# A seventh weight buffer, and one shift column moved behind the shift of tile 12, in a convolution block on one core

## The chip, the cores and the metric

The kernel runs on one core of one Trainium2 chip. The metric is the device time of one execution in microseconds; the time before is the median of three runs. The profile is one more execution, with its own time.

## The reference, cut to what matters

One decoder layer (depth 1, sequence 256, model width 2048) whose mixer is a causal convolution of width 31, with modulation by a conditioning vector `c`:

```python
cond = silu(c)
sh1, sc1, g1, sh2, sc2, g2 = split(cond @ mod_w + mod_b, 6)
h = rms_norm(x, norm1_g) * (1 + sc1) + sh1
a, gt = split(h @ w_in + b_in, 2)                    # "in":  2048 -> 4096
u = depthwise_conv31(a * sigmoid(gt), dw_w) + dw_b
u = silu(layer_norm(u, ln_g, ln_b))
y = u @ w_out + b_out                                # "out": 2048 -> 2048
x = x + (1 + g1) * y
h = rms_norm(x, norm2_g) * (1 + sc2) + sh2
x = x + (1 + g2) * (square(relu(h @ mlp_w1)) @ mlp_w2)   # "up", "down"
```

All is float32. The kernel multiplies matrices in three passes of a rounded high part and a low part (`hi`, `lo`).

## The kernel before, in words

**Tiles and jobs.** Channels lie on the 128 partitions, 16 tiles of 128 channels, and the 256 tokens lie along the free axis. The matrix work is a list `jobs`: 16 input jobs `("in", i)`, each of which gives one tile `u[i]` (an `a` half and a gate half), 8 output jobs, and the MLP in four quarters of 8 `up` and 8 `down` jobs. In the profile input jobs 8 to 15 end at about 279 us and output job 0 starts at about 304 us. The first eight input jobs run in the opening stage beside the modulation columns.

**Weights.** Every 1 MB weight block is loaded into one of `RAW` buffers named `raw` (128x2048, f32). ACT rounds it to `hi` (L206), and DVE or POOL subtracts to get `lo` (L209). The splits of the input jobs and of the early output block `("out", 1, 0)` go to POOL, those of most others to DVE.

**Modulation.** One `mod_w` block serves either as a row load, `raw<-mod_r`, which PE multiplies by the conditioning vector in 8 matmuls (L310), or as a column load, `raw<-mod_c`, which DVE multiplies and sums in one pass over 2048 elements (`mod_col`, L390), or in two halves (L386) once the output stage has begun. `cols_in` are the first `COLS_IN` columns of the second shift; `late` is the list of the other late rows and columns, dealt to jobs by `LATE_IN` and `LATE_OUT` in `after[job]`.

**Order of loads.** SP issues all loads in one hand-written list `order` (`todo`, `top_up`): for each job the weights of the next job and then what `after` holds for it; at input job 15 it also holds `parts_early` behind that job's successor. `room` bounds how far the list runs ahead of the program, and a load waits in SP's queue until its `raw` buffer is free.

**The convolution.** Eight of the sixteen tiles (`PE_TILES`) are convolved on PE as small diagonal matmuls (`pe_conv`, L735) from a rearranged copy `wide` (`copy_wide`, L710 on DVE and L712 on ACT, nine and seven copies for tiles 14 and 15); the others are taps on DVE (L627), joined by `join` (L630). A common shift is taken out of the convolved tiles before their squares are summed (`add_shift`, L674).

**The end of the input stage (job 15).** The program writes, in this order: the two columns of `cols_in`, held behind the last `join`; the matmuls of job 15; the gate of tile 15 (sigmoid on ACT at L750, product on DVE at L752); its nine and seven copies; the shift of tile 12 (`cvs[3][:, 0:1]`); conv 14 and its statistics (L680); two modulation rows; conv 15; the rest of the statistics; the other seven rows; and then the LayerNorm. For each of eight pairs of tiles the LayerNorm subtracts the mean on POOL (L897), scales on DVE (L898), does the silu on ACT (L902) and splits the result into `hl` (L217 on ACT, and L219 and L220 on DVE). Output job 0 takes these pairs in order as they come. `state["e_end"]` is the DVE instruction behind which columns and DVE's splits of the output weights are put.

Of the kernel before, what the change touches and what calls it, by code (L numbers as in the profile page):

```python
# [11 lines left out]
ALU = mybir.AluOpType  # L12
# [5 lines left out]
KT = D // P  # L18
# [19 lines left out]
ROWS = [nb for g in GROUPS for nb in g]  # L38
COLS = [w * KT + k for k in range(KT) for w in (SC1, SH1)]
COLS += [w * KT + k for w in (SH2, G2) for k in range(KT)]  # L40
RAW = 6
FIRST = 4
PE_TILES = (0, 1, 2, 9, 10, 12, 14, 15)
CONV_AT = {9: (0,), 10: (1,), 11: (2,), 12: (9,), 13: (10,), 14: (12,), 15: (14,)}
ADVANCE = {7: 24, 8: 34, 9: 34, 10: 34, 11: 34, 12: 32, 13: 37, 14: 99}
SHIFT = 2
COPY_AT = {8: 0, 9: 1, 10: 2, 11: 9, 12: 10, 13: 12}
PADDING = 784
UNSHIFTED = 7
LATE_IN = [0] * 8 + [4, 4, 4, 4, 4, 3, 0, 9]  # L50
AHEAD = 2
LATE_OUT = [1, 1, 2, 2, 3, 3, 1, 1]
COLS_IN = 2
URGENT = 400
HELD = 8
EARLY_U = 5
# [10 lines left out]
def conv_block(ctx: ExitStack, tc: tile.TileContext, x, vec, dwq, c_row, mod_r, mod_c, w_first, w_in, w_out, w1, w2, out):  # L67
    nc = tc.nc
# [41 lines left out]
    for i in range(2):  # L110
        p = ps.tile([P, 2, 2 * T], F32, name="mm", bufs=2)
        for n in range(2):
            at = 8 * i + 4 * n
# [4 lines left out]
    state = {"used": 0}  # L118
# [20 lines left out]
    waiting = {"raw": 0, "first": 0, "vec": 0, "x": 0}  # L139
    room = {"raw": RAW + 1, "first": FIRST + 1, "vec": 1, "x": 0}  # L140
    todo = []
# [21 lines left out]
    def home(key):  # L163
        return key[0] if key[0] in ("first", "x", "vec") else "raw"

    def top_up():
        while todo and waiting[home(todo[0])] < room[home(todo[0])]:
            key = todo.pop(0)
            tag = home(key)
            waiting[tag] += 1  # L170
            if tag == "raw":
                raw[key] = wts.tile([P, KT, P], F32, name="raw", bufs=RAW)
            elif tag == "first":
                raw[key] = start_pool.tile([P, 2 * HELD, P], F32, name="first", bufs=FIRST)
            elif tag == "x":
                raw[key] = x_pool.tile([P, KT, T], F32, name="x1")
            else:
                raw[key] = v[:, soon:]
                with tc.issue_after(state["load"].ins):
                    state["load"] = nc.sync.dma_start(dwq_sb, dwq)  # L180
            with tc.issue_after(state["load"].ins) if "load" in state else ExitStack():
                if key in SPLIT_LOADS:
                    first_half = nc.sync.dma_start(raw[key][:, 0:HALF], source(key)[:, 0:HALF])
                    with tc.issue_after(first_half.ins):
                        state["load"] = nc.sync.dma_start(raw[key][:, HALF:], source(key)[:, HALF:])
                else:
                    state["load"] = nc.sync.dma_start(raw[key], source(key))

    def take(key):
        assert order[state["used"]] == key, (order[state["used"]], key)  # L190
        state["used"] += 1
        waiting[home(key)] -= 1
        top_up()
        return raw.pop(key)
# [181 lines left out]
        if which in amps:  # L376
            in_order(lambda: nc.vector.tensor_tensor(amps[which][:, k : k + 1], accs[0], col("n1g", k), op=ALU.mult))

    def mod_col(at):
        w = take(("col", at)).rearrange("p k n -> p (k n)")  # L380
        which, k = divmod(at, KT)
        acc = modc[:, at : at + 1]
        if which == SH2 and "cond" in state:
            n = HALF * P
            for half, total in zip(state["cond"], (acc, rest2[:, k : k + 1])):
                nc.vector.scalar_tensor_tensor(w[:, 0:n], w[:, 0:n], 1.0, half, op0=ALU.mult, op1=ALU.mult, accum_out=total)  # L386
                w = w[:, n:]
            return
        with tc.issue_after(state["e_end"]) if "e_end" in state else ExitStack():
            nc.vector.scalar_tensor_tensor(w, w, 1.0, cb, op0=ALU.mult, op1=ALU.mult, accum_out=acc)  # L390
        if which in amps:
            return nc.vector.scalar_tensor_tensor(
                amps[which][:, k : k + 1], acc, col("modb", at), col("n1g", k), op0=ALU.add, op1=ALU.mult
            )
        elif which != SH2:
            return mod_bias(at, 1, acc)

    def mods(keys):
        for key in keys:
            if key[0] == "mod":  # L400
                mod_chunk(*key[1:])
            else:
                mod_col(key[1])
# [60 lines left out]

    late = [("mod", nb, kg) for nb in ROWS for kg in range(4)] + [("col", SH2 * KT + k) for k in range(COLS_IN, KT)]
    cols_in = [("col", SH2 * KT + k) for k in range(COLS_IN)]
    last = [("col", G2 * KT + k) for k in range(KT)]
# [7 lines left out]
    quota = {("in", i): n for i, n in enumerate(LATE_IN)}  # L475
    quota.update({("out", i): LATE_OUT[i] for i in range(HALF)})
    after = {}
    for job in jobs:
        n = quota.get(job, 0)
        after[job], late = late[:n], late[n:]  # L480
        if job == ("in", KT - 1):
            after[job] = cols_in + after[job]
        if job[:2] in LATE_GATE:
            n = LATE_GATE[job[:2]][job[2]]
            after[job], last = last[:n], last[n:]
# [38 lines left out]
    p = ps.tile([P, 512], F32, name="small", bufs=1)  # L524
    for k2 in range(HALF):
        s = two()
# [8 lines left out]
    with urgent():  # L535
        part = two()[:, 0, :]
        nc.scalar.activation(part, p[:, 0:T], AF.Copy)
        p = ps.tile([P, 512], F32, name="row", bufs=1)
# [8 lines left out]
    for _ in range(2):  # L547
        p = ps.tile([P, 2, 2 * T], F32, name="mm", bufs=2)
# [31 lines left out]
    for k in range(KT):  # L580
# [4 lines left out]
        if c == 0:  # L585
            n = two()
# [18 lines left out]
    cvs = [cvp.tile([P, 4, T], F32, name=f"cv{i}") for i in range(4)]  # L605
# [21 lines left out]
            nc.vector.scalar_tensor_tensor(out, s, w, acc, op0=ALU.mult, op1=ALU.add)  # L627

    def join(out, acc, s):
        state["joined"] = nc.vector.tensor_tensor(out, acc, s, op=ALU.add).ins  # L630

    def conv_steps(ct):
        acc = ps.tile([P, 2, T], F32, name="acc", bufs=2)
# [37 lines left out]

    def add_shift(tiles, n):
        by = state["small"][:, None, T : 2 * T].to_broadcast([P, n, T])
        nc.vector.tensor_tensor(tiles, tiles, by, op=ALU.add)  # L674

    def sum_round(pairs, first=False, last=()):
        for n, tiles in enumerate(zip(*pairs)):
# [38 lines left out]
    def make_diag(ct):  # L716
        diags[ct] = cp.tile([P, 32, 32], F32, name="diag", bufs=2)
        at = PE_TILES.index(ct)
        with tc.issue_after(state["pool"]):
            nc.gpsimd.tensor_tensor(  # L720
                diags[ct],
                col("same", 0, 32)[:, None, :].to_broadcast([P, 32, 32]),
                dwq_sb[:, 32 * at : 32 * at + 32][:, :, None].to_broadcast([P, 32, 32]),
                op=ALU.mult,
            )
# [50 lines left out]
    for n, job in enumerate(jobs):  # L776
        if n < HELD:
            continue
        for ct in CONV_AT.get(n, ()) + ((15,) if n == KT - 1 else ()):
            make_diag(ct)  # L780
        if n < len(jobs) - 1:
            splits(jobs[n + 1])
        if n in COPY_AT:
# [5 lines left out]
        kind, i = job[0], job[-1]  # L789
        if kind == "out" and i > 0:  # L790
            p = ps_two()
        elif not by_tokens(job):
            p = ps.tile([P, 2, 2 * T], F32, name="mm", bufs=2)
# [3 lines left out]
        if job == ("up", 0, 0):  # L797
            mm(p, 0, job + (0,), xa, range(SIDE))
            for at in range(2 * UNSCALED):
                shift_row(at, shown.pop(("up", 0, at // 2, at % 2)))  # L800
            fold_shift()
            mm(p, 0, job + (0,), xa, range(SIDE, KT))
            mm(p, 1, job + (1,), xa)
        elif job in K_OUTER:
            for k2 in range(HALF):
                for c in range(2):
                    mm(p, c, job + (c,), xa if plain else hl, range(2 * k2, 2 * k2 + 2), kind == "out")
        elif kind == "in":
            rows = list(after[job]) if i < KT - 1 else []
            if i == KT - 1:  # L810
                state["e_end"] = state["joined"]
                mods(cols_in)
            for c in range(2) if i < KT - 1 else (1, 0):
                for ks in (range(HALF), range(HALF, KT)):
                    mm(p, c, job + (c,), hl, ks, i == KT - 1)
                    with tc.issue_after(state["mm_end"].ins):
                        mods(rows[:1])
                    del rows[:1]
        elif by_tokens(job):
            mm_tokens(sums[kind, i // 2], job, u2 if kind == "down" else hl, n == len(jobs) - 1)  # L820
        else:
            for c in range(2):
                mm(p, c, job + (c,), hl, merged=kind == "out")
        mod_finish()
        if kind == "in":
# [7 lines left out]
            if n == KT - 2:  # L833
                add_shift(cvs[2][:, 1:3, :], 2)
            if n == KT - 1:
                add_shift(cvs[3][:, 0:1, :], 1)
            for ct in CONV_AT.get(n, ()):
                with tc.issue_after(state["mm_end"].ins):
                    mix(ct)
# [7 lines left out]
            sq15 = two()  # L847
            with tc.issue_after(state["conv_end"].ins):
                stats(2)
            rows = after[job][COLS_IN:]  # L850
            with tc.issue_after(state["stats_end"].ins):
                mods(rows[:AHEAD])
            del rows[:AHEAD]
# [39 lines left out]
            for k2 in range(HALF):  # L893
                e = two()
                f = ps_two()
                with urgent():
                    nc.gpsimd.tensor_tensor(e, pair_of(cvs, k2), spread(mu), op=ALU.subtract)  # L897
                    state["e_end"] = nc.vector.tensor_tensor(e, e, spread(r), op=ALU.mult).ins  # L898
                    for c in range(2):
                        k = 2 * k2 + c  # L900
# [10 lines left out]
            pad = ctx.enter_context(tc.tile_pool(name="pad", bufs=1, side="right"))  # L911
            pad.tile([P, PADDING], F32, name="pad")
            mp = ctx.enter_context(tc.tile_pool(name="mlp", bufs=1, side="right"))
# [5 lines left out]
        if kind == "out":  # L919
# [4 lines left out]
            with urgent():  # L924
                for c in range(2):
                    k = 2 * i + c
# [10 lines left out]
            for c in range(2):  # L937
                k = 2 * i + c
# [27 lines left out]
        elif kind == "up":  # L966
# [3 lines left out]
            if plain:  # L970
                with urgent():
# [3 lines left out]
                    for c in range(2):  # L975
                        at = 2 * i + c
# [13 lines left out]
        else:  # L990
# [13 lines left out]
            for t, cs, p in sums.pop((kind, i // 2)):  # L1004
                at = slice(512 * (i // 2) + cs.start, 512 * (i // 2) + cs.stop)
                s = y[:, t, at]
# [71 lines left out]
```

## Time and profile before

| | us |
|---|---|
| three runs | 1107.52, 1106.05, 1105.78 |
| median | 1106.05 |
| the profiled execution | 1107.45 |
| its span | 1105.7 |
| PE busy | 1086.5 (98%) |
| DVE busy | 746.9 (68%) |
| ACT busy | 509.3 (46%) |
| POOL busy | 194.4 (18%) |
| mean DMA rate | 284 GB/s |

The span is what the profiler recorded between the first and the last instruction; 1.75 us of the profiled execution's time lie outside it. All times in the profile count from the start of the span. PE's work is pipelined, so its busy share says that it nearly always has something to do. The number in brackets at the end of a timeline row is the idle time of the engine ahead of that row, and the instruction that ended it. Engines are PE (matmuls), DVE (vector), ACT (activations), POOL (GpSimd) and SP, which issues the loads.

### The profile page before, as it was taken

What the parts mean: (1) busy time and instruction counts of PE and PEld (TensorE: products, weight loads), DVE (VectorE), ACT (ScalarE), POOL (GpSimd) and SP (SyncE); (2) the same over time, 40 slices, a digit from 0 to 9 for tenths busy, and PEclk for the clock granted to TensorE, in tenths of its full rate; (3) what the DMA queues carried; (4) which work ended last, traced back from release to release, by engine and by line L of the source; (5) the groups of instructions that cost most, each with busy time, mean ns of one, the idle gap of its engine ahead of it and who ended that gap; (6) DMA issues with size and microseconds to landing.
All of it is one profiled execution on the core that took longest, in us unless ns stands there. A gap on an engine that the chain in (4) does not pass through costs nothing.

```text
span 1105.7 us, 15404 instructions
## 1 busy us (share of the span) xinstructions
PE 1086.5 (98%) x6018; PEld 892.9 (81%) x6018; DVE 746.9 (68%) x1023; ACT 509.3 (46%) x679; POOL 194.4 (18%) x119
## 2 busy tenths in 40 slices
PE   7999999999899999999999999999999999999998
PEld 4888876668499998888888888888888888888887
DVE  5777789989666966667875666645656665565653
ACT  4111296664576587444444444433444433444431
POOL 0000176468669343000000000000000000000000
PEclk9999999999999999999999999999999999999999
DMA  9999999976899967889996888857898967788631
GB/s 384 420 421 421 416 375 353 353 287 248 329 362 382 396 242 231 254 270 301 357 412 214 227 255 264 305 153 271 252 237 238 251 204 216 227 240 247 208 105 39
DMA packets 142315, 314.23 MB, mean 284 GB/s; under 512 B 87585, under 2 KB 105505, under 8 KB 107297
## 3 DMA queue, kind: packets, MB, share of 16 engines
q1 hardware_dynamic: 142096, 313.11, 81.0%
q8 instruction: 47, 0.77, 0.3%
q14 instruction: 26, 0.21, 0.1%
q10 hardware_dynamic: 146, 0.13, 0.0%
HBM read 301.15 MB, written 12.07 MB: 283 GB/s over the span
## 4 chain that ended last, share of the span: by engine, by line
PE 85%; DMA 10%; DVE 3%; issue 1%; ACT 0%; SPq 0%; DVEq 0%; ACTq 0%
PE mm L258 20%; PE mm L257 20%; PE mm L259 20%; DMA raw<-mod_c 9%; PE mm L234 6%; PE mm L235 3%; PE acc L231 2%; PE acc L230 2%; PE acc L232 2%; PE row L310 2%; DVE raw L390 2%; PE mm L735 2%; DMA raw<-mod_r 1%; DVE wide L710 1%; DMA x<-x 1%; PE mm L562 1%
## 5 line engine op out<-in xcount | busy, mean ns | idle before, releaser
L206 ACT ACTIVATE hi<-raw 128x1024 fp32r<-128x1024 f32 x320 | 334.9, 1057 | 360.8 <-PE mm L259 324.1
L209 DVE TENSOR_TENSOR lo<-raw,hi 128x1024 fp32r<-128x1024 f32 x257 | 312.0, 1223 | 176.9 <-ACT hi L206 176.3
L258 PE MATMUL mm<-lo,u 128*128 128x512 f32 x496 | 193.0, 389 | 0.0
L257 PE MATMUL mm<-hi,u 128*128 128x512 f32 x496 | 193.0, 389 | 0.0
L259 PE MATMUL mm<-hi,u 128*128 128x512 f32 x496 | 192.9, 389 | 0.0
L209 POOL TENSOR_TENSOR lo<-raw,hi 128x1024 fp32r<-128x1024 f32 x63 | 155.2, 2489 | 199.8 <-ACT hi L206 196.2
L259 PE MATMUL mm<-hi,hl 128*128 128x512 f32 x480 | 186.7, 389 | 0.0
L258 PE MATMUL mm<-lo,hl 128*128 128x512 f32 x480 | 186.7, 389 | 0.0
L257 PE MATMUL mm<-hi,hl 128*128 128x512 f32 x480 | 186.7, 389 | 0.0
L390 DVE SCALAR_TENSOR_TENSOR raw<-raw,cond 128x2048 f32<-128x2048 f32 x51 | 122.6, 2407 | 63.2 <-DMA raw<-mod_c 63.2
L259 PEld LDWEIGHTS mm<-hi,u 128*128 128x128 f32 x496 | 93.1, 188 | 19.3
L258 PEld LDWEIGHTS mm<-lo,u 128*128 128x128 f32 x496 | 93.1, 188 | 19.0
L257 PEld LDWEIGHTS mm<-hi,u 128*128 128x128 f32 x496 | 93.1, 188 | 19.1
L259 PEld LDWEIGHTS mm<-hi,hl 128*128 128x128 f32 x480 | 90.1, 188 | 18.7
L257 PEld LDWEIGHTS mm<-hi,hl 128*128 128x128 f32 x480 | 90.1, 188 | 18.7
L258 PEld LDWEIGHTS mm<-lo,hl 128*128 128x128 f32 x480 | 90.1, 188 | 18.7
L627 DVE SCALAR_TENSOR_TENSOR acc<-u,v,acc 128x256 f32<-128x256 f32 x224 | 94.4, 485 | 1.8
L234 PE MATMUL mm<-hl,hi 128*128 128x512 f32 x224 | 81.5, 405 | 0.0
L562 PE MATMUL mm<-two,first 128*128 128x256 f32 x256 | 60.1, 389 | 8.4 <-ACT two L593 8.3
L562 PEld LDWEIGHTS mm<-two,first 128*128 128x128 f32 x256 | 49.1, 194 | 18.2 <-ACT two L593 11.5
L230 PE MATMUL acc<-hl,hi 128*128 128x256 f32 x224 | 63.4, 283 | 0.0
L231 PE MATMUL acc<-hl,hi 128*128 128x256 f32 x224 | 63.4, 283 | 0.0
(183 smaller groups left out, 1281.1 us busy)
## 6 DMA issues: line engine op xcount, KB each, us to landing
raw<-w SPq DMA_DIRECT2D x128, 1024.0 KB, 5.4
raw<-mod_c SPq DMA_DIRECT2D x62, 1024.0 KB, 9.4
raw<-mod_r SPq DMA_DIRECT2D x32, 1024.0 KB, 7.7
raw<-w_in SPq DMA_DIRECT2D x16, 1024.0 KB, 7.1
raw<-w_out SPq DMA_DIRECT2D x16, 1024.0 KB, 7.9
first<-w_first SPq DMA_DIRECT2D x15, 1024.0 KB, 19.8
flat<-two SPq DMA_DIRECT2D x30, 256.0 KB, 2.8
two<-flat SPq DMA_DIRECT2D x120, 64.0 KB, 4.2
```

Of the source, the lines that this page charges most:

```text
L206: state["w_hi"] = nc.scalar.activation(hi, w[:, ks, :], AF.Copy).ins
L209: end = by.tensor_tensor(lo, w[:, ks, :], hi.bitcast(F32), op=ALU.subtract)
L230: nc.tensor.matmul(out_p, w, m[:, 0:T], start=begin, stop=False)
L231: nc.tensor.matmul(out_p, w, m[:, T : 2 * T], start=False, stop=False)
L234: nc.tensor.matmul(p[:, c, :], hi[:, k % HALF, :], m, start=(k == 0), stop=(k == KT - 1))
L235: state["mm_end"] = nc.tensor.matmul(p[:, c, T : 2 * T], lo[:, k % HALF, :], m[:, 0:T], start=False, stop=(k == KT - 1), skip_group_check= ...
L257: nc.tensor.matmul(p, p_hi, hi, start=begin, stop=False)
L258: nc.tensor.matmul(p, p_hi, lo, start=False, stop=False)
L259: nc.tensor.matmul(p, p_lo, hi, start=False, stop=end)
L390: nc.vector.scalar_tensor_tensor(w, w, 1.0, cb, op0=ALU.mult, op1=ALU.mult, accum_out=acc)
L562: step = nc.tensor.matmul(held[n][:, c, :], w[:, 2 * n + c, :], h, start=k == 0 and c == 0, stop=k == KT - 1, skip_group_check=True)
L627: nc.vector.scalar_tensor_tensor(out, s, w, acc, op0=ALU.mult, op1=ALU.add)
```

## The change

The dynamic scratch of the program is cut from 4096 to 256 bytes and `PADDING` from 784 to 720, and `RAW` goes from 6 to 7. `COLS_IN` goes from 2 to 1, so that the second of the two columns goes to the list `late`; `LATE_OUT` takes it up at output job 3. The remaining column's load moves from the list of input job 15 to the end of that of input job 14, which puts it ahead of the loads of the output weights. Job 15 claims the loaded block early (`taken`), and its product is written behind the shift of tile 12, after which `e_end` also stands.

```diff
-RAW = 6
+RAW = 7
-PADDING = 784
+PADDING = 720
-LATE_OUT = [1, 1, 2, 2, 3, 3, 1, 1]
-COLS_IN = 2
+LATE_OUT = [1, 1, 2, 3, 3, 3, 1, 1]
+COLS_IN = 1
...
-    def mod_col(at):
-        w = take(("col", at)).rearrange("p k n -> p (k n)")
+    def mod_col(at, w=None):
+        w = (take(("col", at)) if w is None else w).rearrange("p k n -> p (k n)")
...
-        if job == ("in", KT - 1):
-            after[job] = cols_in + after[job]
+        if job == ("in", KT - 2):
+            after[job] = after[job] + cols_in
...
     def join(out, acc, s):
-        state["joined"] = nc.vector.tensor_tensor(out, acc, s, op=ALU.add).ins
+        nc.vector.tensor_tensor(out, acc, s, op=ALU.add)
...
     def add_shift(tiles, n):
...
-        nc.vector.tensor_tensor(tiles, tiles, by, op=ALU.add)
+        return nc.vector.tensor_tensor(tiles, tiles, by, op=ALU.add).ins
...
+        if n == KT - 1:
+            taken = [(key, take(key)) for key in cols_in]
         if n < len(jobs) - 1:
             splits(jobs[n + 1])
...
-            rows = list(after[job]) if i < KT - 1 else []
-            if i == KT - 1:
-                state["e_end"] = state["joined"]
-                mods(cols_in)
+            rows = [key for key in after[job] if key not in cols_in] if i < KT - 1 else []
...
             if n == KT - 1:
-                add_shift(cvs[3][:, 0:1, :], 1)
+                state["e_end"] = add_shift(cvs[3][:, 0:1, :], 1)
+                for key, w in taken:
+                    mod_col(key[1], w)
...
-            rows = after[job][COLS_IN:]
+            rows = list(after[job])
...
-    nc = bacc.Bacc("TRN2", target_bir_lowering=False, num_devices=1, dynamic_dma_scratch_size=4096)
+    nc = bacc.Bacc("TRN2", target_bir_lowering=False, num_devices=1, dynamic_dma_scratch_size=256)
```

## The prediction

> **What bounds the kernel now.** I read the page first, for the engines and the chain that ended last, then that chain over 255 to 320 us, the only place after the conditioning stage where something other than TensorE (PE) ends it; then the timelines of the engines there.
>
> ```profile
> span 1105.7 us, 15404 instructions
> ```
> ```profile
> PE 1086.5 (98%) x6018; PEld 892.9 (81%) x6018; DVE 746.9 (68%) x1023; ACT 509.3 (46%) x679; POOL 194.4 (18%) x119
> ```
> ```profile
> PE 85%; DMA 10%; DVE 3%; issue 1%; ACT 0%; SPq 0%; DVEq 0%; ACTq 0%
> ```
>
> PE carries 85% of the chain; nearly all of the DMA share is the stage of modulation columns at the start, whose loads and their order the change leaves alone. What can be won is idle time of PE. The chain, sorted by time, at the end of the input jobs:
>
> ```profile
> 279.17 4.47 DVE raw L390 x3
> ...
> 293.73 8.60 DMA raw<-mod_r
> 302.37 1.93 PE row L310 x8
> ```
>
> Two things hold PE: two column products (L390) ahead of the shift and the gate of job 15, and the last row load, issued at 293.73 and landed 8.60 later. The idle time itself, in PE's timeline (start, busy, line, idle ahead in brackets):
>
> ```profile
> 284.03 0.41 PE L680 MATMUL small<-cv,ones 128*32 128x256 f32 x2 [1.11 <-DVE cv L674]
> ...
> 284.92 1.90 PE L310 MATMUL row<-raw,cz 128*32 128x512 f32 x16
> 286.75 0.70 PE L732 MATMUL acc<-shift,v 128*128 128x256 f32 x2
> 287.69 4.39 PE L735 MATMUL acc<-wide,diag 128*32 128x256 f32 x63 [0.24 <-ACT wide L712]
> ...
> 295.58 3.64 PE L310 MATMUL row<-raw,cz 128*32 128x512 f32 x32
> 299.76 1.06 PE L310 MATMUL row<-raw,cz 128*32 128x512 f32 x8 [0.55 <-DMA raw<-mod_r]
> 302.37 1.93 PE L310 MATMUL row<-raw,cz 128*32 128x512 f32 x8 [1.54 <-DMA raw<-mod_r]
> ...
> 315.11 0.28 PE L230 MATMUL acc<-hl,hi 128*128 128x256 f32 x1
> ```
>
> The windows of the same stretch give PE's busy time, and after the engines the granted clock, the DMA share and GB/s:
>
> ```profile
> 302.40:306.00 3.60, 3.60 (x16) 1.94 (x17) 3.60 (x7) 3.10 (x7) 3.60 (x4) 0.53 1.05 446
> 306.00:315.00 9.00, 9.00 (x78) 9.00 (x77) 4.37 (x7) 8.80 (x15) 2.31 (x2) 1.00 0.99 413
> ```
>
> After the two waits for rows PE ran 3.6 us at 0.53 of its clock, which cost 3.6 x 0.47 = 1.7 us of work. From 306 on I found no stall of PE up to the end, so what out job 0 ends earlier than at 315.11 stays won, if nothing behind it becomes late.
>
> **The column and the copies of tile 15.** Job 15 now starts with one column instead of two, and the shift of tile 12 (L674) stands ahead of it.
>
> ```profile
> 274.78 4.46 DVE L390 SCALAR_TENSOR_TENSOR raw<-raw,cond 128x2048 f32<-128x2048 f32 x1
> ...
> 279.17 4.46 DVE L390 SCALAR_TENSOR_TENSOR raw<-raw,cond 128x2048 f32<-128x2048 f32 x1
> ...
> 283.56 0.41 DVE L674 TENSOR_TENSOR cv<-cv,small 128x256 f32<-128x256 f32 x1
> 283.90 0.47 DVE L752 SCALAR_TENSOR_TENSOR u<-mm,v,two 128x256 f32<-128x256 f32 x1
> 284.40 4.19 DVE L710 COPY wide<-u 32x284 f32<-32x284 f32 x9
> ```
> ```profile
> 274.69 2.40 POOL L209 TENSOR_TENSOR lo<-raw,hi 128x1024 fp32r<-128x1024 f32 x1 [1.50 <-ACT hi L206]
> 277.51 8.37 POOL L209 TENSOR_TENSOR lo<-raw,hi 128x1024 fp32r<-128x1024 f32 x2 [0.42 <-ACT hi L206]
> ```
> ```profile
> 385.27 2.29 DVE L390 SCALAR_TENSOR_TENSOR raw<-raw,cond 128x2048 f32<-128x2048 f32 x1
> ```
> ```profile
> 280.22 0.46 ACT L750 ACTIVATE two<-mm,v 128x256 f32<-128x256 f32 x1
> ```
>
> A column alone takes 2.29; here each took 4.46, since the two engines took turns: POOL to 277.09, column, POOL's first half of out (1, 0), column, POOL's second half to 285.88. With one column: L674 at 274.8 to 275.2 (it ran 0.41 beside POOL, so POOL does not hold it); the column waits for POOL until 277.1 and ends near 279.2, as its first did; POOL's first half runs 279.2 to 281.55. The gate needs the sigmoid, done at 280.68, and ends at 281.1 instead of 284.37. That is 3.3 us for the gate. The copies do not get it all:
>
> ```profile
> 265.57 7.80 DVE L710 COPY wide<-u 32x284 f32<-32x284 f32 x9
> ```
>
> Nine copies of tile 14, among POOL's splits and diagonals, took 7.80; nine of tile 15 took 4.19, of which the first waited for POOL's end at 285.88 and the rest ran in 2.5 us. The Trainium skill, "SBUF — State Buffer", section "Who interferes with whom", says that VectorE and GpSimd share one port pair as an exclusive lock, that a VectorE copy or a two-input operation waits out a GpSimd instruction which reads, and that issue order decides. By that rule alone the copies lose to POOL's second half; the trace agrees (4.46 against 2.29). So I let POOL's second half go first, 281.55 to 284.0 with one copy perhaps slipped in between; the eight or nine that are left take 2.5 to 2.8 and end at 286.5 to 286.8, where before they ended at 284.40 + 4.19 = 288.59. Gain for conv 15: 1.8 to 2.1; I take 1.95. If the copies won against POOL they would end near 284.4 and PE would decide: no wait for L674 (1.11), no 0.24, and no waiting inside conv 15 (63 matmuls took 4.39, where 64 of tile 14 took 3.66, so about 0.8): 2.2 at most. The lower bound is 0: in that case the copies wait for POOL twice, 2.4 more.
>
> ACT's seven copies of the tile are not last: in PE's row above ACT ended the wait at 287.69, 3.3 after the gate, so they would be done at 284.4.
>
> **The row loads.** The seventh buffer, and a column's load that no longer stands at the head of the nine row loads, let each of these go out at an earlier release.
>
> ```profile
> 285.91 8.15 SPq L187 DMA_DIRECT2D raw<-mod_r  x4
> ```
>
> The last four went out from 285.91 on, the ninth at 293.73, when row 3 had been consumed. After the change the ninth waits for row 2's matmuls, which end at 286.7 before and 1.1 earlier after: 285.7 (rows 1 and 2 are the 16 matmuls from 284.92). The loads ahead of it have moved up as well; the DMA moves 420 GB/s, 2.5 us for 1.05 MB, so the ninth lands between 288.2 and, at worst, the landing of the eighth before, near 299.7. PE would want the ninth at 295.58 + 3.64 + 0.91 - 1.95 = 298.2. So both waits go (2.1 us); at the worst bound 1.5 stays, most of it in time in which PE then waits for the LayerNorm anyway.
>
> **What is late next: the LayerNorm.** Out job 0 consumes seven pairs of tiles as they come. Its pace is set by DVE's last pass of each pair:
>
> ```profile
> 301.45 0.69 DVE L220 TENSOR_TENSOR hl<-acc,hl 128x512 fp32r<-128x512 f32 x1 [0.69 <-ACT hl L217]
> ...
> 309.88 0.69 DVE L220 TENSOR_TENSOR hl<-acc,hl 128x512 fp32r<-128x512 f32 x1
> ```
>
> A pair is 12 matmuls of 0.12 us (9.00 us hold some 75 of them), 1.44. The sixth pair is ready at 310.57; it and the seventh then need 2.88, so the LayerNorm alone would have let PE end at 313.45, against 315.11. The difference, 1.66, is the half-clock stretch to within 0.1: without it, PE would have done row nine in 0.91 instead of 1.9 (it ended it near 304.3) and ended the seven pairs at 313.4 too, in spite of the waits. So the rows' waits are worth 1.66 in this execution, and no more, and only because they bring the clock down. Beyond that only conv 15, which the statistics and the LayerNorm follow, moves the end: 313.45 - 1.95 = 311.5.
>
> Sum for the profiled execution: 315.11 - 311.5 = 3.6. Its time is 1107.45 (span 1105.7 and 1.75 around it), so 1103.85. The runs before are 1107.52, 1106.05 and 1105.78: the profiled one is 1.40 above the median, about the price of the half-clock stretch, which I take the median not to have. From the median only the 1.95 comes off: 1104.1. Forecast: **1103.9**.
>
> **What costs nothing.** The scratch cut only frees memory: every queue of the page is hardware-fed, and no DMA is issued by POOL. The third column at out job 3 is two half products (1.21 each) on a DVE that is 68% busy. It replaces the 4.46 of job 15; at worst it pushes DVE by 2.4 in a stage without stalls of PE.
>
> **Rivals.** *Only the clock is won.* The copies wait for two POOL instructions, or something else in conv 15's chain stays. For: tile 14's 7.80. Against: POOL has nothing left after 284.0, since its next split follows the LayerNorm. Gain from the profile 1.66: 1105.8. Chance 0.14.
>
> *The clock falls again.* PE now ends row nine at about 299.15, and the first pair is ready at 302.14 - 1.95 = 300.2; further waits of about 0.9 and 0.3 follow in out job 0. That is 2.2 us idle again, though spread over 9 us; 1.35 us at 283 to 288 cost no clock before, 2.1 within 3.2 did. Price at most 1.7, part of it inside LayerNorm waits: 1104.3 to 1105.6. The Trainium skill, "TensorE: Matmul & The Clock Gate", section "What's actually happening", has a free-running window of 3413 ns, so whether a stretch counts as idle depends on where the window falls; the slow stretch here lasted about that long. Chance 0.12.
>
> *All of 3.6 comes off the median*, if that holds the half-clock stretch too: 1102.4. Chance 0.14.
>
> *The MLP's columns come late: slower.* With seven buffers a weight and a column change places at two quarters, and a DVE product that waits for its load holds up what is queued behind it:
>
> ```profile
> 495.47 2.29 DVE L390 SCALAR_TENSOR_TENSOR raw<-raw,cond 128x2048 f32<-128x2048 f32 x1 [3.88 <-DMA raw<-mod_c]
> ...
> 497.69 1.31 DVE L270 STREAM_TRANSPOSE two<-mm 128x512 f32<-128x512 f32 x2
> ```
> ```profile
> 502.60 0.39 PE L257 MATMUL mm<-hi,u 128*128 128x512 f32 x1
> ```
>
> The transposes end at 499.0 and free the sum that PE writes at 502.60: 3.6 us of slack. It decides from a column that lands over 3.6 later than now; one 1 MB load ahead of it costs 2.5, two cost 5.0, so 1.4 per place, and with a like wait in each of two quarters up to 2.8 beyond a lost gain: 1107 to 1109. Against: with more buffers loads go out earlier, not later. Chance 0.08.
>
> *The change does not do what it says*: releases come in the same order with the column still ahead of the row loads, the time stays 1106. Chance 0.04.
>
> **How the numbers follow.** The forecast has 0.48. What a measurement of this kernel tells from no change is about 0.2%, 2.2 us, which puts the border at 1103.84, in the middle of the forecast's 1103.5 to 1104.3. Since the kernel before itself sits at 1107.5 as often as at 1105.9 in four executions, a comparison sees 2.0 or 3.6, mostly over the border: of 0.48 I count 0.42 as faster; with 0.14, 0.56. Same: 0.06 + 0.14 + 0.12 + 0.04, less 0.02 for slower tails: 0.34. Slower: 0.08 + 0.02. The range runs from 1102.3 (3.6 off the median) to 1106.1 (nothing).
>
> **What would show it.** In the profile after: L674 ahead of one L390 near 275; the gate's end near 281; copies of tile 15 in two parts around a POOL split, the last near 286.6; no wait of L310 for mod_r; conv 15 1.9 earlier; out job 0's second sums at 311.5; the clock at 1.00 around 302. Wrong if the last copy ends after 288, if a row is still waited for past 300, or if PE shows a new wait after 320.

## The result and the profile after

The changed kernel takes 1103.72 us (median of 10 runs, 1103.37 to 1103.96), the kernel before, run beside it, 1105.93 (10 runs, 1105.77 to 1107.54). The ratio, taken over all these runs, is 0.9976, with a 95% interval of 0.9966 to 0.9986. The ratio of the two medians is 0.9980, since three of the ten runs before took 1107.1 to 1107.5. The forecast was 1103.9. The change lies at the prediction's border of 0.2%: just beyond it by the ratio, on it by the medians, and the interval includes it. The profiled execution after took 1103.93, with a span of 1102.1 us.

The page's parts on the span and on the chain that ended last, after:

```profile
span 1102.1 us, 15388 instructions
```
```profile
PE 88%; DMA 9%; DVE 2%; ACT 1%; issue 0%; SPq 0%; ACTq 0%
```

DVE's timeline after, at the start of input job 15, and POOL's beside it:

```profile
274.88 0.41 DVE L674 TENSOR_TENSOR cv<-cv,small 128x256 f32<-128x256 f32 x1
275.21 4.14 DVE L390 SCALAR_TENSOR_TENSOR raw<-raw,cond 128x2048 f32<-128x2048 f32 x1
...
280.82 0.49 DVE L752 SCALAR_TENSOR_TENSOR u<-mm,v,two 128x256 f32<-128x256 f32 x1 [1.46 <-ACT two L750]
281.34 5.06 DVE L710 COPY wide<-u 32x284 f32<-32x284 f32 x9
```
```profile
277.62 6.38 POOL L209 TENSOR_TENSOR lo<-raw,hi 128x1024 fp32r<-128x1024 f32 x2 [0.41 <-ACT hi L206]
```

The gate ends at 281.31 where it ended at 284.37. The nine copies take longer than before (5.06 against 4.19), since POOL's second half lies among them until 284.00, and end at 286.40 instead of 288.59. The first copy gets in ahead of that half; the second waits for its end. PE's timeline:

```profile
286.17 3.71 PE L735 MATMUL acc<-wide,diag 128*32 128x256 f32 x63
...
293.40 5.36 PE L310 MATMUL row<-raw,cz 128*32 128x512 f32 x48
299.30 0.38 PE L230 MATMUL mm<-hl,hi 128*128 128x256 f32 x1 [0.54 <-ACT hl L217]
300.02 0.39 PE L231 MATMUL mm<-hl,hi 128*128 128x256 f32 x1 [0.34 <-DVE hl L220]
...
302.42 0.38 PE L231 MATMUL mm<-hl,hi 128*128 128x256 f32 x1 [0.69 <-DVE hl L220]
...
311.31 0.28 PE L230 MATMUL acc<-hl,hi 128*128 128x256 f32 x1
```

Conv 15 runs its 63 matmuls without a wait inside (3.71, before 4.39). L745, the DVE instruction that follows conv 15, before and after:

```profile
292.33 0.48 DVE L745 TENSOR_SCALAR cv<-acc,v 128x256 f32<-128x256 f32 x1 [3.22 <-PE small L680]
```
```profile
290.13 0.48 DVE L745 TENSOR_SCALAR cv<-acc,v 128x256 f32<-128x256 f32 x1 [3.22 <-PE acc L735]
```

All 48 matmuls of the last six rows follow one another. PE now waits for the LayerNorm alone, and output job 1 starts at 311.31 instead of 315.11. The windows, with the granted clock third from the end, show no half-clock stretch:

```profile
300.00:303.00 3.00, 2.28 (x17) 2.08 (x18) 3.00 (x6) 2.54 (x5) 3.00 (x4) 1.00 0.93 393
303.00:306.00 3.00, 3.00 (x28) 3.00 (x27) 2.51 (x5) 2.90 (x6) 1.12 (x1) 1.00 1.00 423
```

From there to the last matmul the two traces run in parallel: the same matmul stands 3.80 us earlier after the change at 315 and at 1095 us. So the difference between the two profiled executions is made between 275 and 311 us. Two small amounts lie outside that stretch: the trace after is already 0.10 late at 275 us, from the opening stage, and its end behind the last matmul is 0.2 longer, so that the spans differ by 3.6.

### The profile page after: what moved, and what is told of

The parts are those of the page before. It is cut to its first block, busy times and chain, and to the rows that moved or that the text cites. A ratio compares the mean times of both kernels' runs of the same rounds, so it can differ in the third digit from the quotient of the medians.

```text
span 1102.1 us, 15388 instructions
## 1 busy us (share of the span) xinstructions
PE 1085.5 (98%) x6018; PEld 892.8 (81%) x6018; DVE 746.3 (68%) x1025; ACT 510.2 (46%) x679; POOL 192.7 (17%) x119
## 4 chain that ended last, share of the span: by engine, by line
PE 88%; DMA 9%; DVE 2%; ACT 1%; issue 0%; SPq 0%; ACTq 0%
PE mm L258 20%; PE mm L257 20%; PE mm L259 20%; DMA raw<-mod_c 9%; PE mm L234 6%; PE mm L235 3%; PE acc L232 2%; PE acc L231 2%; PE acc L230 2%; PE mm L735 2%; PE row L310 2%; DVE raw L390 1%; PE mm L231 1%; DMA x<-x 1%; PE mm L230 1%; PE mm L232 1%
## 5 line engine op out<-in xcount | busy, mean ns | idle before, releaser
L206 ACT ACTIVATE hi<-raw 128x1024 fp32r<-128x1024 f32 x320 | 335.6, 1058 | 367.9 <-PE mm L259 333.6
L390 DVE SCALAR_TENSOR_TENSOR raw<-raw,cond 128x2048 f32<-128x2048 f32 x50 | 118.2, 2366 | 39.8 <-DMA raw<-mod_c 39.6
L232 PE MATMUL acc<-hl,lo 128*128 128x256 f32 x224 | 63.5, 283 | 0.0
L235 PE MATMUL mm<-hl,lo 128*128 128x256 f32 x224 | 63.4, 283 | 0.0
```

The lines of the kernel that those rows point to most:

```text
L206: state["w_hi"] = nc.scalar.activation(hi, w[:, ks, :], AF.Copy).ins
L232: state["mm_end"] = nc.tensor.matmul(out_p, lo[:, k % HALF, :], m[:, 0:T], start=False, stop=end)
L235: state["mm_end"] = nc.tensor.matmul(p[:, c, T : 2 * T], lo[:, k % HALF, :], m[:, 0:T], start=False, stop=(k == KT - 1), skip_group_check= ...
```

## The experiments

Times are medians; the second time is that of the kernel before, run beside them. Ratios are taken over all runs. Theory 1 is the prediction's (the gate and copies of tile 15, then the LayerNorm); theory 2 says that the earlier loads are the gain; theory 3, that it is the shift ahead of the column.

**e1_seven: memory alone.** Buffers, padding and scratch change together here; they were not run apart.

```diff
 (kernel before)
-RAW = 6
+RAW = 7
-PADDING = 784
+PADDING = 720
...
-    nc = bacc.Bacc(..., dynamic_dma_scratch_size=4096)
+    nc = bacc.Bacc(..., dynamic_dma_scratch_size=256)
```

> The kernel before with seven buffers, 256 bytes of scratch and the smaller padding; both columns stay where they were. Theory 1 (what counts is when the gate of tile 15 and its copies come, since conv 15 and the LayerNorm follow them; the row waits cost time only when they pull the clock down): the shift still waits for two columns, PE still waits about 1.1 for L674, the last copy still ends near 288.6, the ninth row goes out near 286.9 and lands near 299.7, so L310 waits 0.5 at most and the clock stays at 1.00; 1105.8, with no run at 1107.5. Theory 2 (the loads are the gain: the row waits are what the change removes): 1103.7. Theory 3 (the gain is the shift ahead of the column, PE's 1.1 wait for L674): 1105.8.

Measured: 1107.69 (1107.33 to 1108.34) against 1105.95, ratio 1.0015 (1.0006 to 1.0024). It is slower, which no theory expected. Up to 320 us theory 1 was right: the wait for L674 was 1.1, no row was waited for, and output job 1 started at 313.61. The rest is lost at the change from the output jobs to the MLP. PE, POOL and DVE in this kernel:

```profile
403.94 1.13 PE L410 MATMUL small<-two,ones 128*128 128x256 f32 x4 [1.02 <-ACT two L930]
```
```profile
394.91 6.82 POOL L209 TENSOR_TENSOR lo<-raw,hi 128x1024 fp32r<-128x1024 f32 x2 [3.76 <-ACT hi L206]
```
```profile
396.06 3.41 DVE L209 TENSOR_TENSOR lo<-raw,hi 128x1024 fp32r<-128x1024 f32 x1
399.39 2.37 DVE L960 TENSOR_TENSOR modc<-modc,rest 128x16 f32<-128x16 f32 x1
```

Output jobs 0 to 5 and two early MLP blocks are split on POOL too (`POOLED` in the kernel), besides those named with the kernel before; so POOL's splits at the end of the output jobs belong to both kernels, and what differs is their order. In the kernel before, with six buffers, the scheduler had no DVE split there, POOL's splits came later, and the small sum L960 was short:

```profile
400.03 0.17 DVE L960 TENSOR_TENSOR modc<-modc,rest 128x16 f32<-128x16 f32 x1
```
```profile
400.44 7.55 POOL L209 TENSOR_TENSOR lo<-raw,hi 128x1024 fp32r<-128x1024 f32 x3 [7.79 <-ACT hi L206]
```

With seven, a split and L960 stand beside two POOL splits, take 3.41 and 2.37 instead of 1.2 and 0.17, and the squares that end the output stage come late. Between 375 and 424 us this kernel loses 1.98 more against the changed one. So the seventh buffer by itself cost time here. That it did so through the order which the scheduler chose is read from the traces; no run fixes that order.

**e2_six: the columns alone.** The changed kernel with `RAW = 6`, `PADDING = 784` and a scratch of 4096.

> The changed kernel with six buffers, 4096 bytes of scratch and the old padding: the moved and removed columns alone. Theory 1: conv 15 starts near 286.2 as in the changed kernel; the ninth row goes out after row 3 near 291.5 and lands near 297, before PE wants it at 298.2; 1103.7 to 1104.0. Theory 2: the last row is waited for again by 1 to 2 us and the time is 1105.0 to 1107.5. Theory 3: 1103.7.

Measured: 1103.61 (1103.27 to 1103.86) against 1105.95, ratio 0.9977 (0.9968 to 0.9987). The ninth row was issued at 291.40 and landed at 298.24, later than expected; the waits of PE from 255 us on are these:

```profile
PE mm L231 <- DVE hl L220: 0.7, 1, 0.7
PE row L310 <- DMA raw<-mod_r: 0.6, 1, 0.6
```

A row is waited for again, by 0.6, in time in which PE would wait for the LayerNorm. The seventh buffer adds nothing to the time. With e1_seven, where the rows came in time and the gain did not, theory 2 falls.

**e3_ahead: the column at its old place.**

```diff
 (changed kernel, job 15; join keeps state["joined"] as before)
+                state["e_end"] = state["joined"]
+                for key, w in taken:
+                    mod_col(key[1], w)
             ...
-                state["e_end"] = add_shift(cvs[3][:, 0:1, :], 1)
-                for key, w in taken:
-                    mod_col(key[1], w)
+                add_shift(cvs[3][:, 0:1, :], 1)
```

> The changed kernel with its one column computed where columns stood before, ahead of the shift of tile 12 and behind the join. Theory 1: the column ends near 279.2 and the shift near 279.7, three microseconds before conv 14 ends at 282.8, so nothing waits for it; 1103.7. Theory 2: 1103.7. Theory 3: PE waits for L674 again and the time is 1104.8 or more.

Measured: 1103.76 (1103.36 to 1104.14) against 1105.95, ratio 0.9978 (0.9969 to 0.9987). L674 ran at 279.27, well ahead of conv 14's end. The place of the shift is worth nothing once there is only one column; theory 3 falls.

**e4_two: both columns behind the shift.** The changed kernel with `COLS_IN = 2` and `LATE_OUT` as before.

> The changed kernel with both columns, loaded early and computed behind the shift of tile 12, seven buffers. Theory 1: the shift is early and PE's wait for L674 is gone, but the gate ends only near 284.3 and the last copy near 288.4, so conv 15 and the LayerNorm come as late as before, and L735 waits about 2 us; 1105.5 to 1105.9. Theory 2: rows are in time, 1103.7. Theory 3: the 1.1 us are won, 1104.7 or less.

Measured: 1107.31 (1107.13 to 1107.58) against 1105.95, ratio 1.0011 (1.0002 to 1.0020). Its DVE timeline and its waits:

```profile
283.43 0.47 DVE L752 SCALAR_TENSOR_TENSOR u<-mm,v,two 128x256 f32<-128x256 f32 x1
283.93 4.50 DVE L710 COPY wide<-u 32x284 f32<-32x284 f32 x9
```
```profile
PE acc L735 <- ACT wide L712: 1.2, 1, 1.2
...
PE small L410 <- ACT two L931: 0.8, 1, 0.8
```

The 1.1 us for L674 are gone and come back as 1.2 for the copies: the last copy ends at 288.43, L745 runs at 292.17, and output job 1 starts at 313.32, as theory 1 has it. This trace is 0.15 early against the kernel before already at 275 us, so at L745 nothing is won. The rest, 1.52 between 375 and 424 us, is lost where e1_seven lost, with the same split of 3.41 and sum of 2.37 on DVE: this kernel too has seven buffers and two columns.

**e6_count: two constants.**

```diff
 (kernel before)
-LATE_OUT = [1, 1, 2, 2, 3, 3, 1, 1]
-COLS_IN = 2
+LATE_OUT = [1, 1, 2, 3, 3, 3, 1, 1]
+COLS_IN = 1
```

> The kernel before with two constants changed: one column less in input job 15 and one more in output job 3. Six buffers, 4096 bytes of scratch, the load at the head of the row loads and the product ahead of the shift, all as before. Theory 1 (the second column is the whole cost, by way of the gate and the copies of tile 15): 1103.6 to 1103.9, conv 15 starting near 286.1, as with the moved load. Theory 2 (early loads are needed): the last row is waited for by 1 us or more, 1104.5 to 1105.5. Theory 3 (the shift's place): 1104.8 or more.

Measured: 1103.50 (1103.29 to 1103.74) against 1106.04, ratio 0.9976 (0.9966 to 0.9985). This is the whole gain of the change, by two constants, with six buffers, the old scratch, the load and the product where they were. From 150 us to the last matmul its trace runs beside that of the changed kernel to within 0.03 us, 0.25 to 0.28 earlier throughout. Conv 15 and the last row in its trace:

```profile
285.91 3.71 PE L735 MATMUL acc<-wide,diag 128*32 128x256 f32 x63
...
298.37 1.07 PE L310 MATMUL row<-raw,cz 128*32 128x512 f32 x8 [0.72 <-DMA raw<-mod_r]
```

**e5_none: no column in job 15.** The changed kernel with `COLS_IN = 0` and a third column at output job 2.

> The changed kernel with no column at all in input job 15 (the last one moves on to output job 2). The copies of tile 15 then wait for one POOL half that ends near 282.8 instead of 284.0 and are done near 285.5 instead of 286.4. Theory A (conv 15 now starts when PE has done the two rows ahead of it, so copies decide nothing): the same time, 1103.7. Theory B (the copies and the lock still decide): 0.8 less, 1102.9.

Measured: 1103.53 against 1106.04, ratio 0.9983 (0.9969 to 0.9996); eleven runs lie between 1103.35 and 1103.96, and the profiled one took 1112.68. In it PE waited 6.2 us from 337.0, behind one DVE sum that took 10.98 while POOL worked without a pause:

```profile
329.32 10.98 DVE L220 TENSOR_TENSOR u<-two,u 128x512 fp32r<-128x512 f32 x1
```
```profile
329.61 0.76 POOL L933 TENSOR_TENSOR sqacc<-two 128x256 f32<-128x256 f32 x1
330.31 9.44 POOL L209 TENSOR_TENSOR lo<-raw,hi 128x1024 fp32r<-128x1024 f32 x4
```

The other times do not hold this wait, and the stage around job 15 lies ahead of it. The copies took 4.27 from 281.48, done at 285.75, 0.65 earlier than after the change; conv 15 started at 286.32, no earlier. With one column PE's own work ahead of conv 15 decides, and theory A holds.

**before_again: the kernel before, profiled a second time.**

> The kernel before, unchanged, profiled once more. The claim under test is that its last row wait costs time only through the clock. If this execution takes about 1105.9, the theory expects the same waits (1.1 for L674, about 2 for mod_r) but a clock of 1.00 after 302 and the first sums of output job 1 near 313.4 instead of 315.1. If the clock is not the cause, the two executions have output job 1 starting at the same 315.1. If it takes 1107.5, the clock is again at half and nothing is learnt.

Measured: 1106.04, span 1104.3. Its PE timeline and the window that was at 0.53 in the first profile:

```profile
299.94 1.06 PE L310 MATMUL row<-raw,cz 128*32 128x512 f32 x8 [0.71 <-DMA raw<-mod_r]
302.54 1.07 PE L310 MATMUL row<-raw,cz 128*32 128x512 f32 x8 [1.54 <-DMA raw<-mod_r]
303.54 0.39 PE L230 MATMUL mm<-hl,hi 128*128 128x256 f32 x1
```
```profile
313.70 0.28 PE L230 MATMUL acc<-hl,hi 128*128 128x256 f32 x1
```
```profile
302.40:306.00 3.60, 3.46 (x28) 2.62 (x29) 3.60 (x7) 3.10 (x7) 3.60 (x4) 1.00 1.05 448
```

The waits are those of the first profile (0.71 and 1.54, there 0.55 and 1.54), the clock stays at 1.00, the last row takes 1.07 instead of 1.93, and output job 1 starts 1.41 earlier. The two executions differ by 1.41 in time as well.

**e7_fill: filling PE's waits.**

```diff
 (changed kernel, output job 0; job 1 then skips what is done)
             for k2 in range(HALF):
                 for c in range(2):
                     mm(p, c, job + (c,), ...)
+                if kind == "out" and k2 < FILL:      # FILL = 7
+                    mm(early_p, 0, ("out", 1, 0), hl, range(2 * k2, 2 * k2 + 2), True)
```

> The changed kernel with the first half of output job 1 worked off beside output job 0, pair by pair of the LayerNorm's tiles: 18 matmuls (2.16 us) for each pair instead of 12 (1.44 us). Only PE's order differs. If PE waits for the LayerNorm, as the changed kernel's trace has it (0.34 and 0.69 us waits for L220 at 300 and 302.4), the second wait shrinks from 0.85 to about 0.2 and the time falls by 0.6 to 1103.1. If PE's idle time there costs nothing, 1103.7.

Measured: 1103.73 (1103.33 to 1103.88) against 1106.04, ratio 0.9977 (0.9968 to 0.9986). Inconclusive: the scheduler put the added matmuls behind later pairs only, from 309.75 on, and the wait at the second pair stayed at 0.69.

**f_fill: the same in a fixed order.** e6_count with twelve matmuls of output job 1 put behind the first and second pair by order constraints on PE.

> The kernel before with the two constants changed (one column less in job 15, one more in output job 3), and six matmuls of output job 1 put behind the first and six behind the second pair of the LayerNorm's tiles, in a fixed order on PE. PE's 0.85 at the second pair shrinks to about 0.2: 0.6 less than the two constants alone, 1102.9. If something in the output stage's order changes for the worse, 1103.5 or more, with a new wait of PE after 320.

Measured: 1111.93 (1111.57 to 1113.32) against 1106.01, ratio 1.0049 (1.0037 to 1.0062).

```profile
309.54 0.58 PE L231 MATMUL acc<-hl,hi 128*128 128x256 f32 x1 [7.10 <-DVE hl L221]
```

The added sums use one of the two PSUM buffers named `acc` through which the LayerNorm passes its pairs. It came free only after the seventh pair's split, and PE stood still for 7.1 us. So e7_fill's question stays unanswered: filling needs another PSUM buffer, which was not tried.

**e9_a1_none, f_a1_none, f_a1_none_fill: one row instead of two ahead of conv 15, and no column.** `AHEAD = 1`, `COLS_IN = 0`, with seven buffers and the loose filling, with six buffers, and with six and the fixed filling.

> No column in job 15, one row instead of two ahead of conv 15, and output job 1's first half beside output job 0. With one row less ahead of it PE reaches conv 15 near 285.3, and copies that end near 285.5 let it start there, 0.6 to 0.8 earlier than 286.2; the LayerNorm follows, and with the filled waits the sum is 1.2 to 1.4: 1102.4. If the copies still end near 286.4, conv 15 stays and only the filled waits count: 1103.1. If the ninth row, issued behind row two and so some 4 us later than now, is waited for, the gain is lost to it: 1103.7 or more.

> The kernel before with no column in job 15 (two more in the output jobs) and one row instead of two ahead of conv 15, six buffers. Conv 15 starts near 285.5, 0.6 to 0.8 earlier than with two rows, and the LayerNorm follows: 1102.7 to 1102.9. The ninth row, issued behind row three, lands near 297.5 and holds PE for up to 1 us, which the LayerNorm covers. If the output stage's order changes for the worse, as in the run with seven buffers (2.2 us for ACT's split at 382 and half the clock after it), 1105 or more.

> The same, with the fixed filling of output job 0 by twelve matmuls of output job 1 added. Both gains: 1102.1 to 1102.4. With a new wait after 320, 1103.5 or more.

Measured: 1108.36 (1106.53 to 1108.86), 1107.57 (1106.48 to 1109.07) and 1111.88 (1111.66 to 1112.73), ratios 1.0017 (1.0008 to 1.0026), 1.0011 (1.0002 to 1.0020) and 1.0049 (1.0036 to 1.0061). The local expectation held in the first two: conv 15 started at 285.37 and 285.21, and at 331 us PE stood 0.79 and 0.94 ahead of the changed kernel. Then both lost about 5 us at one place. PE and ACT in f_a1_none:

```profile
384.16 0.39 PE L230 MATMUL acc<-hl,hi 128*128 128x256 f32 x1 [2.17 <-ACT hi L206]
```
```profile
374.89 0.64 ACT L217 ACTIVATE u<-two 128x512 fp32r<-128x512 f32 x1
382.03 1.11 ACT L927 ACTIVATE acc<-acc,gb,modc 128x256 f32<-128x256 f32 x2 [6.50 <-PE acc L232]
383.06 1.99 ACT L206 ACTIVATE hi<-raw 128x1024 fp32r<-128x1024 f32 x2
```

ACT was idle for 6.50 us and then did L927 of the job before ahead of the split that PE needed, so PE waited 2.17 and then ran at half the clock. By 382 us ACT has run 64 of its passes of L206 after the change, and here 60. The order of ACT's list had changed in a job whose number of late columns the edit leaves alone. e5_none, with no column but two rows ahead of conv 15, does not lose this in its other eleven runs; which part of these edits changes the order was not run apart. The third lost its time to the wait of f_fill (7.3 here). No version was found that beats the changed kernel by more than the runs scatter; e6_count equals it.

## Why the prediction was right, and where its steps were off

**The column and the copies: right, at its upper bound.** Predicted 1.95 for conv 15, bounds 0 and 2.2. L745 moved from 292.33 to 290.13: 2.20, and 2.30 with the 0.10 by which the trace after is late at 275 us, a little above the bound. The bound took its waits from the brackets of PE's rows. A bracket counts only idle time. In the trace after, L680 starts 0.18 before the last matmul of conv 14 ends; at the wait before the change that overlap was lost too. So L680 came 1.28 earlier, the 0.10 included, where the bracket said 1.11. The course was as worked out by hand: copies on both sides of POOL's second half, their end at 286.40 where 286.5 to 286.8 was forecast.

The second column held PE in two places, by L674 and by the copies. e4_two removes the first alone and wins nothing at L745, so the copies come last. By PE's rows, early copies alone would still have left the 1.28 for L674; that was not run. One column less removes both. e5_none shows that copies 0.65 earlier still bring no more: PE's own work is then the end of the scale, as the upper bound had it.

The lock that the prediction took from the Trainium skill, "SBUF — State Buffer", section "Who interferes with whom", agrees: copies wait out POOL's split here, and L960, a sum of two inputs, takes 2.37 beside POOL splits and 0.17 without (e1_seven). The Trainium skill says it of copies in a two-port mode, a condition that the prediction left out; no view here shows the mode of these copies.

**The shift ahead of the column: rightly given no price, and needless.** With one column the shift runs at 279.27 even behind it, and the time is the same (e3_ahead, 1103.76).

**The row loads: right in their times, wrong as a reason for the buffer.** The ninth row went out at 285.67, as worked out (285.7), and landed at 296.14, before PE wanted it. The prediction gave the end of the two waits to the seventh buffer and the moved load. The buffer alone does end them (e1_seven). But with six buffers and one column (e2_six, e6_count) only a wait of 0.6 to 0.7 stays, and the time is the same. The sum did not suffer, because it had priced these waits only through the clock. As a reason for the seventh buffer the step fails, and alone that buffer cost 1.7 (e1_seven, 1107.69 against 1105.95).

**The clock: right, with 1.41 for 1.66.** before_again separates it cleanly: same waits, other clock, 313.70 against 315.11. Output job 1 would have started at 313.45 by the LayerNorm alone; the 0.25 between is the cost of the waits themselves, which the prediction put at nothing. e1_seven, without waits for rows, gives 0.22 for it, when the start of its trace is set against that of before_again.

That the median of before lacks the half-clock stretch was also right: of 33 runs of before beside e6_count, 26 lie between 1105.67 and 1106.25 and 7 between 1107.26 and 1107.94. The mean granted clock of each run says that the second group is the half clock. A stretch of 3.6 us at 0.53 lowers the mean over the span by 0.0015. Over the three sets of runs of before beside the experiments (79 runs), the 13 above 1107.2 have 0.995 or 0.998, and the others 0.996, 0.997, 0.999 or 1.00. Against the first group the gain is some 2.2, against the second some 3.7. From four executions the prediction took the second group to be as frequent as the first; it is 13 of 79.

**The forecast: its last 0.2 was luck.** From the median the prediction's sum gives 1104.1. The forecast of 1103.9 lies between that and the 1103.85 of the profiled execution, and no term stands for the difference. By the traces without half clock (before_again and after) PE gained 2.49 in this stage: 2.30 at conv 15, where 1.95 was taken, and 0.2 from the row waits. Take off the 0.10 of the opening stage and the 0.2 behind the last matmul, and 2.2 is left, which is what the medians show.

**What costs nothing: right for the changed kernel, too lightly argued.** The third column at output job 3 cost nothing (3.80 at 315 and at 1095 us). But the prediction held that a stage without stalls of PE takes an edit with little loss, and e1_seven, e4_two, e9_a1_none and f_a1_none lost 1.5 to 5.8 us in just that stage. The rival on the slower side looked in the MLP for loads that come late; the real danger was a changed order of splits at the end of the output jobs. The changed kernel escaped it, and the prediction has no reason why: that was luck.

**The rivals.** Neither *only the clock is won* nor *the change does not do what it says* came about: conv 15 did move, by 2.20. *All of 3.6 off the median* fell with the second profile of before. The clock did not fall again in the changed kernel's profile, and its runs lie within 0.6 us, in one group: PE's waits there are 1.57 us in all, in three pieces. By the Trainium skill, "TensorE: Matmul & The Clock Gate", section "What's actually happening", the window is free-running; that the same waits of 2.1 to 2.3 us brought half the clock in one execution and not in another agrees with this. The longest of these waits was 1.54 us, so no such window stood idle as a whole.

## What to carry to other kernels

Find the one engine whose late work the next stage hangs on, and take away work ahead of it: here one vector product of 2.3 us, which took 4.46 beside another engine's splits, was the whole gain, and a buffer, a new load order and a new place added nothing to it. Try the parts of a bundled change alone; one part can be a loss that another hides. Where a scheduler orders the instructions, look after every edit at the engines' order in the stages that the edit does not touch.

## What was not expected of the hardware

A wait of PE can cost more than its length, and not in every execution: two waits that sum to 2.1 us in one execution and 2.3 in the other were followed by 3.6 us at 0.53 of the clock in the first and by full clock in the second, 1.41 us apart. A DVE sum on 16 columns took 2.37 us instead of 0.17 beside POOL's splits, and ended with the last of them (401.76 against 401.73, e1_seven). In one execution a DVE sum of 0.7 us stood beside five POOL instructions in a row, took 10.98, and ended 0.55 after the last of them (e5_none); in the other eleven runs of that kernel the time shows no such wait.
